# One packed load for seven small inputs, weight splits and a count moved off GpSimd, and the last norms on VectorE

## The chip, the cores and the metric

The kernel runs on 1 core of one Trainium2 chip. A core has five engines that work side by side: PE (TensorE, matrix products), DVE (VectorE), ACT (ScalarE), POOL (GpSimd) and SP (SyncE, which here only starts DMA transfers). Each engine takes its instructions strictly in order; semaphores make one wait for another. Transfers are started from the queues of SP, ACT and POOL. The metric is the device time of the whole program in microseconds; lower is better. The time before is the median of three runs, 4089.68 us, between 4086.54 and 4090.18.

## The reference, cut to what matters

The input is 2048 tokens of 1024 numbers and a condition vector. The program computes one layer of a network. `_layer_norm` is (x − mean)·rsqrt(var + eps).

```python
m = split(silu(c) @ mod_w + mod_b, 6)                       # six rows of 1024
h = _layer_norm(x, 1e-6) * (1 + m[1]) + m[0]
y = _hyena(h, ...)                                          # projection, short and long convolutions, w_out
x = _ln_affine(alpha * x + (1 + m[2]) * y, ln_g[0], ln_b[0])
h = _layer_norm(x, 1e-6) * (1 + m[4]) + m[3]
aff = softmax(h @ w_router)                                 # 2048 x 16
gate, idx = top_k(aff.T, 256)                               # each of 16 experts picks 256 tokens
ye = (silu(xe @ w1) * (xe @ w3)) @ w2 * gate                # xe = h[idx], inner width 2048
x = _ln_affine(alpha * x + (1 + m[5]) * scatter_add(ye), ln_g[1], ln_b[1])
```

The filters of the long convolution come out of a small network with sine activations (`hy_f_w1`, `hy_f_b1`, `hy_f_freq`, ...), and their spectra are needed.

## The kernel before

The program runs through stages on one core. From 0 to some 120 us (the **start**) it forms the first two rows of the modulation (`early_mod`): SP loads 16 tiles `mw` of 128x1024; the products of five of the eight tiles of one half run on PE as columns of `sd` (L462), the rest is accumulated on DVE in `macc` (L467) and summed over partitions by `sd<-ones_f,macc` on PE (L470); L473 adds the bias `mb` and gives `md`, which stands on DVE ahead of the last statistics of the first quarter of the tokens. A tile `mw` has a buffer that PE or DVE must free before SP loads the next into it. Beside it `filter_acts` runs the sine network: products `sp`, `g` (L209), `turn` on ACT (L211), the rounding `kk` on DVE (L213, L214), and the sine `a` or `zt` on ACT (L215). `side_steps` loads the tokens in quarters of 4 tiles, adds the position rows on POOL, takes the statistics on DVE (L376), and `rstd_steps` (L380 to L393) makes 1/sqrt(var + eps): `lva` on DVE, the root on ACT, a Newton step on DVE; `norm` scales the four tiles on ACT (L506). PE then transposes them (L522) and the projection of `_hyena` begins. An order of the instructions at the start is chosen by a scheduler from the code's order and waits.

Then come filters, projection and convolutions up to some 1510 us, and `phase_out` (the product with `w_out`, the norms, the logits of the router) to some 1772, in 20 rounds `n`, written by hand. Beside it `moe_start` is a generator: its first step builds constants and loads the first chunk of the first expert's weights; its second step, run at `n == 16` of `phase_out`, derives `tri` and `blkb`; its third, run in `phase_route` after the exponentials, splits two chunks.

A **split** is how single precision is kept with the faster matmul type: a weight tile (`w1r`, `w3r`, `w2r`, 128x2048 a chunk) is cast to a high half on ACT (`w1h`), and a low half is the difference (`w1l`) from DVE, or at the first two chunks from POOL (L1400, L1401). Each product is then three matmuls.

`phase_route` (L1274) picks the 256 tokens of each expert by a search for the threshold: 15 steps, 7 on the upper and 8 on the lower 16 bits of the weights. A step counts with three DVE instructions (L1320, `junk`, the count in `cnt`) how many of 128x256 values reach three candidates; PE sums the counts over partitions (`cp`, L1322); DVE compares (L1338), and forms the next candidates (`base` L1335, `cand` L1342, `thr` L1324).

`phase_moe` (L1440) then runs the experts. `route(e)` (L1452) finds the indices, gathers 2x128 tokens (`xg`) and transposes them through the PSUM buffer `tp` (one buffer) into `xs` in two halves; `project` makes `ab` (three buffers), `hidden` the product with silu (`u`, `hh`, `hl`), `back` the accumulation `acc`. Experts 0 to 12 are ordered by the scheduler. The **last three experts** (some 3640 to 4065 us) have their order written by hand: each has 16 steps `n` of `project_summed`, `flush` (the `back` of the step before), `hidden`, the splits for the next chunk (two on even steps, one on odd ones), and one turn of each open `settle`. A `settle` takes 256 tokens of the sum of all experts (`accd`), gathered or straight, and does their final norm; the table `plan` says at which step of which expert one opens. Ten are opened. Its steps are: load; nothing; statistics, `va` and the start value of 1/sqrt (L1565 to L1570) on DVE and three Newton rounds on POOL (L1572 to L1577); and the scaling, per 128 tokens one ACT instruction (L1580) and two POOL instructions by `ln_g` and `ln_b` (L1581, L1582). The last expert's own tokens are normed by code at the end that the change leaves alone.

## Time and profile before

| | |
|---|---|
| median of 3 runs | 4089.68 us (4086.54 to 4090.18) |
| profiled execution | 4085.04 us, span 4083.2 us |
| mean granted clock of TensorE | 0.975 |
| busy: PE, DVE, ACT, POOL | 94%, 68%, 48%, 25% |
| chain that ended last: PE, DVE, issue, DMA, POOL, ACT | 75%, 9%, 5%, 4%, 3%, 3% |

The chain is followed back from the last instruction to what released each step. As PE is busy nearly throughout, an instruction of another engine counts only where PE waits for it, and the views by stretch and by wait tell where that is. Times are microseconds from the start of the span unless marked ns.

### The profile page before, as it was taken

To read this page: it belongs to the slowest core of one execution; us is meant where nothing else is said; L and a number is where in the kernel's file an instruction comes from. 1 tells how busy PE (TensorE), PEld (TensorE's weight loads), DVE (VectorE), ACT (ScalarE), POOL (GpSimd) and SP (SyncE) were. 2 spreads that over 40 slices of the span, in tenths; PEclk is the share of its full clock that TensorE was granted. 3 is DMA by queue.
4 is the path that set the end of the run, shared out by engine and by line. 5 is a ranking of instruction groups with operands and counts; after the bars stand their busy time and mean duration, and the time that the engine had idled before them with its cause. 6 is when DMAs were issued, how large, how long until landed. Compare 5 with 4: busy or idle time off the path is not lost.

```text
span 4083.2 us, 52931 instructions
## 1 busy us (share of the span) xinstructions
PE 3833.0 (94%) x19839; PEld 3171.7 (78%) x19839; DVE 2789.9 (68%) x4017; ACT 1940.8 (48%) x2845; POOL 1040.3 (25%) x1092
## 2 busy tenths in 40 slices
PE   4899999999999989939999999999999999999997
PEld 3666766777777877827888888888888888888896
DVE  5777876776877877785666666666666666656766
ACT  3544543333777651114555555555555555544443
POOL 2355552212455442220000000000000000014635
PEclk8999999999999999969999999999999999999999
...
GB/s 201 113 175 173 179 172 210 221 205 227 268 283 278 294 251 203 136 162 167 196 193 209 206 196 188 214 204 195 188 215 203 195 189 213 203 176 221 238 228 159
DMA packets 620796, 831.73 MB, mean 204 GB/s; under 512 B 56627, under 2 KB 506947, under 8 KB 618236
## 3 DMA queue, kind: packets, MB, share of 16 engines
...
q10 hardware_dynamic: 17858, 2.95, 0.5%
...
q14 instruction: 100, 0.82, 0.1%
...
## 4 chain that ended last, share of the span: by engine, by line
PE 75%; DVE 9%; issue 5%; DMA 4%; POOL 3%; ACT 3%; SPq 0%; ACTq 0%; POOLq 0%; DVEq 0%
PE ab L1502 19%; PE ab L1503 10%; PE acc L175 5%; PE acc L176 5%; PE acc L177 5%; PE ip L175 3%; PE ip L177 3%; PE ip L176 3%; PE sp L335 2%; PE xp L854 2%; PE ap L889 2%; PE xp L872 2%; PE op L175 1%; PE op L177 1%; PE op L176 1%
## 5 line engine op out<-in xcount | busy, mean ns | idle before, releaser
L1502 PE MATMUL ab<-xs,w3h 128*128 128x512 f32 x1664 | 600.6, 399 | 0.0
L1502 PE MATMUL ab<-xs,w1h 128*128 128x512 f32 x1664 | 598.2, 399 | 0.0
L1401 DVE TENSOR_TENSOR w2l<-w2r,w2h 128x2048 fp32r<-128x2048 f32 x126 | 297.6, 2362 | 267.0 <-ACT w2h L1400 266.9
L1503 PE MATMUL ab<-xs,w3l 128*128 128x256 f32 x1664 | 468.2, 281 | 0.0
L1503 PE MATMUL ab<-xs,w1l 128*128 128x256 f32 x1664 | 466.6, 280 | 0.0
L175 PE MATMUL acc<-w2h,hh 128*128 128x512 f32 x1024 | 404.1, 395 | 14.3 <-ACT hh L170 13.8
L176 PE MATMUL acc<-w2l,hh 128*128 128x512 f32 x1024 | 402.5, 393 | 0.0
L177 PE MATMUL acc<-w2h,hl 128*128 128x512 f32 x1024 | 399.5, 391 | 0.8 <-DVE hl L171 0.8
L1502 PEld LDWEIGHTS ab<-xs,w3h 128*128 128x128 f32 x1664 | 313.0, 188 | 76.6
L1502 PEld LDWEIGHTS ab<-xs,w1h 128*128 128x128 f32 x1664 | 313.0, 188 | 72.9
...
L1401 DVE TENSOR_TENSOR w1l<-w1r,w1h 128x2048 fp32r<-128x2048 f32 x126 | 301.0, 2389 | 62.7 <-ACT w1h L1400 62.6
L170 ACT CAST hh<-u 128x256 fp32r<-128x256 f32 x256 | 104.1, 407 | 478.6 <-DVE u L1525 478.6
L1503 PEld LDWEIGHTS ab<-xs,w1l 128*128 128x128 f32 x1664 | 314.2, 189 | 7.1
L1506 DVE TENSOR_TENSOR u<-ab,u 128x256 f32<-128x256 f32 x416 | 174.6, 420 | 205.2 <-ACT u L1505 196.8
L1503 PEld LDWEIGHTS ab<-xs,w3l 128*128 128x128 f32 x1664 | 314.8, 189 | 0.0
L1401 DVE TENSOR_TENSOR w3l<-w3r,w3h 128x2048 fp32r<-128x2048 f32 x126 | 292.9, 2324 | 18.7 <-ACT w3h L1400 18.7
L1400 ACT CAST w2h<-w2r 128x2048 fp32r<-128x2048 f32 x128 | 244.1, 1907 | 94.7 <-PE acc L177 86.3
L1400 ACT CAST w1h<-w1r 128x2048 fp32r<-128x2048 f32 x128 | 244.5, 1910 | 80.5 <-PE ab L1502 79.0
L1400 ACT CAST w3h<-w3r 128x2048 fp32r<-128x2048 f32 x128 | 244.5, 1910 | 68.4 <-PE ab L1502 66.3
L1505 ACT COPY u<-ab 128x256 f32<-128x256 f32 x416 | 152.8, 367 | 184.9 <-PE ab L1503 184.8
L175 PE MATMUL ip<-hh,wh 128*128 128x512 f32 x576 | 237.4, 412 | 3.3 <-ACT hh L170 3.3
...
## 6 DMA issues: line engine op xcount, KB each, us to landing
w1r<-in_moe_w_dram SPq DMA_DIRECT2D x128, 1024.0 KB
w3r<-in_moe_w_dram SPq DMA_DIRECT2D x128, 1024.0 KB
w2r<-in_moe_w_dram SPq DMA_DIRECT2D x128, 1024.0 KB
fud<-ev SPq DMA_DIRECT2D x128, 256.0 KB
...
bn<-ao POOLq DMA_DIRECT2D x248, 128.0 KB, 7.2
...
```

What stands on the lines that cost most here:

```text
L170: nc.scalar.copy(hi, raw)
L175: nc.tensor.matmul(out, lhsT=ah, rhs=bh, start=start, stop=False)
L176: nc.tensor.matmul(out, lhsT=ah, rhs=bl, start=False, stop=False)
L177: nc.tensor.matmul(out, lhsT=al, rhs=bh, start=False, stop=stop)
L335: nc.tensor.matmul(p, lhsT=s1[:, th], rhs=hb[th], start=True, stop=(n0 > 0))
L854: nc.tensor.matmul(p[:, i], lhsT=s2[:, 2 * gp + i], rhs=r[:, i], start=True, stop=True)
L1400: nc.scalar.copy(h, raw)
L1401: eng.tensor_tensor(l, raw, f_(h), OP.subtract)
L1502: nc.tensor.matmul(p, lhsT=ws[2 * j][:, k, fs], rhs=xs[:, k], start=(k == 0), stop=False)
L1503: nc.tensor.matmul(p[:, 0], lhsT=ws[2 * j + 1][:, k, fs], rhs=xs[:, k, 0], start=False, stop=(k == 7))
L1505: nc.scalar.copy(u, p[:, 1])
L1506: nc.vector.tensor_tensor(u, p[:, 0], u, OP.add)
```

## The change

It has seven parts.

1. The inputs `c`, the first 2048 of `mod_b`, `hy_conv_w`, `hy_conv_b`, `hy_b_in`, `hy_f_freq`, `hy_f_b1` and `hy_f_b2` are packed by the host into one array of 128x148, loaded by one SP transfer (`small`). The SP loads `cs` and `mb`, six `fb` loads and three `prm` loads on the ACT queue go.
2. `rstd_steps` takes the root on ACT straight from the variance with the eps as a bias, and its Newton step has four instructions with three fused ones, and `nb`; the rounding difference `kk` is now a fused instruction.
3. In `phase_out` the second step of `moe_start` comes at `n == 17`, and with it the load of the table for Exp; that step now casts `w1h`, `w3h` on ACT and subtracts `w1l`, `w3l` on DVE. The split of `w2` and that of the second chunk come when the tokens of expert 0 have been gathered and transposed, on ACT and DVE. POOL splits nothing.
4. In a step of the search the third count is made on ACT as a sum of signs (`cs`), DVE makes two, and the comparison is against a row of limits (`lim`).
5. For expert 0 `route(0, wide=True)` transposes three of its four groups into the `ab` buffers.
6. `settle` does everything but transfers on DVE, in five steps: load; nothing; statistics; Newton and the first 128 tokens' two scalings; the second 128 tokens' two scalings.
7. In `plan`, the third settle of the first of the last experts opens at step 6 instead of 5.

The core of the diff:

```diff
 def rstd_steps(nc, wk, r, nb, stat, eps, n):
 
-    va = wk.tile([128, n], F32, name="lva")
-    nc.vector.tensor_scalar(va, stat[:, :, 1], eps, None, op0=OP.add)
+    nc.scalar.activation(r, stat[:, :, 1], AF.Sqrt, bias=eps)
+    yield 1
     sq = wk.tile([128, n], F32, name="lsq")
-    nc.scalar.activation(sq, va, AF.Sqrt)
-    yield 1
-    nc.vector.reciprocal(r, sq)
-    nc.vector.tensor_tensor(sq, r, r, OP.mult)
-    nc.vector.tensor_tensor(sq, sq, va, OP.mult)
-    nc.vector.tensor_scalar(sq, sq, -0.5, 1.5, op0=OP.mult, op1=OP.add)
-    nc.vector.tensor_tensor(r, r, sq, OP.mult)
+    nc.vector.reciprocal(r, r)
+    nc.vector.scalar_tensor_tensor(sq, stat[:, :, 1], eps, r, op0=OP.add, op1=OP.mult)
+    nc.vector.scalar_tensor_tensor(sq, sq, -0.5, r, op0=OP.mult, op1=OP.mult)
+    nc.vector.scalar_tensor_tensor(r, sq, 1.5, r, op0=OP.add, op1=OP.mult)
     nc.vector.scalar_tensor_tensor(nb, stat[:, :, 0], -1.0, r, op0=OP.mult, op1=OP.mult)
     yield 1
...
-            if n == 16:
+            if n == 17:
+                nc.scalar.activation(wk.tile([128, 1], F32, name="r"), ident[:, 0:1], AF.Exp)
                 next(nxt)
             if n < 16:
...
-                cnt = wk.tile([128, 3], BF16, name="cnt", bufs=2)
-                for k in range(3):
+                cnt = wk.tile([128, 2], BF16, name="cnt", bufs=2)
+                cs = wk.tile([128, 1], BF16, name="cs", bufs=2)
+                sign = wk.tile([128, 256], BF16, name="sign")
+                with nc.allow_low_precision(reason="whole numbers of at most 256"):
+                    nc.scalar.activation(sign, v, AF.Sign, scale=-1.0, bias=cand[:, 2:3], accum_out=cs)
+                for k in range(2):
                     junk = wk.tile([128, 256], U16, name=f"junk{k}")
-                    nc.vector.tensor_scalar(junk, v, cand[:, k:k + 1], 0.0, op0=OP.is_ge, op1=OP.add, accum_out=cnt[:, k:k + 1])
+                    nc.vector.tensor_scalar(junk, v, cand[:, k:k + 1], 0.0, op0=OP.is_lt, op1=OP.add, accum_out=cnt[:, k:k + 1])
                 p = ps.tile([128, 3], F32, name="cp", bufs=2)
-                nc.tensor.matmul(p, lhsT=blkb, rhs=cnt, start=True, stop=True)
+                nc.tensor.matmul(p[:, 2:3], lhsT=blkb, rhs=cs, start=True, stop=True)
+                nc.tensor.matmul(p[:, 0:2], lhsT=blkb, rhs=cnt, start=True, stop=True)
                 if n == steps[0]:
                     nc.vector.memset(t, 0.0)
...
     nc.gpsimd.iota(ii, pattern=[[1, 128]], base=128, channel_multiplier=-1)
     yield
+    hs = [(n, raw, wt.tile(list(raw.shape), F32R, name=n + "h"), wt.tile(list(raw.shape), F32R, name=n + "l")) for n, raw in raws]
+
+    def sub(i):
+        _, raw, h, l = hs[i]
+        nc.vector.scalar_tensor_tensor(l, raw, 1.0, f_(h), op0=OP.mult, op1=OP.subtract)
+
+    for i in range(2):
+        nc.scalar.copy(hs[i][2], hs[i][1])
+    for i in range(2):
+        sub(i)
     nc.vector.tensor_scalar(R.tri, ii, 128.0, None, op0=OP.is_gt)
     nc.vector.tensor_scalar(ii, ii, 15, None, op0=OP.bitwise_and)
     nc.vector.tensor_scalar(R.blkb, ii, 0.0, None, op0=OP.is_equal)
+    R.first = [t for h in hs for t in h[2:]]
     yield
-    R.first = []
-    for n in range(2):
-        R.first.append(split(raws, nc.gpsimd))
-        if n == 0:
-            raws = load(0, 1)
+    nc.scalar.copy(hs[2][2], hs[2][1])
+    yield
+    sub(2)
+    raws = load(0, 1)
+    R.second = split(raws[:2])
+    R.raw = raws[2:]
     yield
 
...
             for q in range(4):
-                p = ps.tile([128, 2, 256], F32, name="tp", bufs=1)
+                p = ps.tile([128, 2, 256], F32, name="ab", bufs=3) if wide and q else ps.tile([128, 2, 256], F32, name="tp", bufs=1)
                 for i in range(2):
                     k = 2 * q + i
...
+            yield
             va = wk.tile([128, 2], F32, name="va2")
             nc.vector.tensor_scalar(va, stat[:, :, 1], LN_EPS, None, op0=OP.add)
             r = wk.tile([128, 2], F32, name="r2")
-            nb = wk.tile([128, 2], F32, name="nb2")
             t = wk.tile([128, 2], F32, name="t2")
             nc.vector.tensor_scalar(t.bitcast(I32), va.bitcast(I32), 1, None, op0=OP.logical_shift_right)
             nc.vector.tensor_scalar(r.bitcast(I32), t.bitcast(I32), -1.0, float(0x5f3759df), op0=OP.mult, op1=OP.add)
             for _ in range(3):
-                nc.gpsimd.tensor_tensor(t, r, r, OP.mult)
-                nc.gpsimd.tensor_tensor(t, t, va, OP.mult)
-                nc.gpsimd.tensor_scalar(t, t, -0.5, 1.5, op0=OP.mult, op1=OP.add)
-                nc.gpsimd.tensor_tensor(r, r, t, OP.mult)
-            nc.gpsimd.tensor_scalar(nb, stat[:, :, 0], -1.0, None, op0=OP.mult)
-            nc.gpsimd.tensor_tensor(nb, nb, r, OP.mult)
-            yield
+                nc.vector.scalar_tensor_tensor(t, r, -0.5, r, op0=OP.mult, op1=OP.mult)
+                nc.vector.tensor_tensor(t, t, va, OP.mult)
+                nc.vector.scalar_tensor_tensor(r, t, 1.5, r, op0=OP.add, op1=OP.mult)
             for j in range(2):
-                nc.scalar.activation(x[:, j], x[:, j], AF.Identity, scale=r[:, j:j + 1], bias=nb[:, j:j + 1])
-                nc.gpsimd.tensor_tensor(x[:, j], x[:, j], gb[:, 0], OP.mult)
-                nc.gpsimd.tensor_tensor(x[:, j], x[:, j], gb[:, 1], OP.add)
+                if j:
+                    yield
+                nc.vector.scalar_tensor_tensor(x[:, j], x[:, j], stat[:, j, 0:1], gb[:, 0], op0=OP.subtract, op1=OP.mult)
+                nc.vector.scalar_tensor_tensor(x[:, j], x[:, j], r[:, j:j + 1], gb[:, 1], op0=OP.mult, op1=OP.add)
                 if idx is not None:
                     nc.gpsimd.indirect_dma_start(out=out[0], out_offset=at(idx, j), in_=x[:, j], in_offset=None)
             if idx is None:
                 nc.gpsimd.dma_start(dst, x)
...
-        plan = {-3: {1: "xh", 3: "xl", 5: "xh"}, -2: {0: "xh", 2: "-xl", 5: "xh"}, -1: {0: "xh", 2: "-xl", 5: "xh", 7: "xl"}}
+        plan = {-3: {1: "xh", 3: "xl", 6: "xh"}, -2: {0: "xh", 2: "-xl", 5: "xh"}, -1: {0: "xh", 2: "-xl", 5: "xh", 7: "xl"}}
```

**ACT at the start.** Before, the three loads of `prm` stand on ACT between the third `turn` and the first sine `a`:

```order
L211 ACTIVATE turn<-g,frq 128x512
L211 ACTIVATE turn<-sp,frq 128x512
L593 DMA prm<-in_hy_conv_w_dram 128x72x1
L594 DMA prm<-in_hy_conv_b_dram 128x24x1
L595 DMA prm<-in_hy_b_in_dram 128x24x1
L215 ACTIVATE a_459<-kk 128x512 x2
```

Now (with buffer numbers, since some rows read alike without them):

```order
L205 DMA fw3_118<-in_hy_f_w2_dram 64x64 x2
L215 ACTIVATE turn_449<-sp_447,frq_133 128x512
L215 ACTIVATE turn_457<-g_455,frq_133 128x512
L215 ACTIVATE turn_465<-sp_463,frq_133 128x512
L219 ACTIVATE a1_446<-kk_451 128x512
L215 ACTIVATE turn_473<-g_471,frq_133 128x512
```

The sine follows `turn` with no load between them.

**PE at the start**, between the modulation's columns and the sums over partitions. Before (`sd<-sg,mw` are columns of the modulation, `fw` the weights of the sine network):

```order
L462 MATMUL sd<-sg,mw 128x1 x8
L209 MATMUL sp<-a_459,fw_119 128x512
L209 MATMUL g<-a_459,fw_119 128x512
L470 MATMUL sd<-ones_f,macc_170 128x1 x8
L470 MATMUL sd<-ones_f,macc_171 128x1 x8
L209 MATMUL sp<-zt,fw_120 128x512
```

Now:

```order
L459 MATMUL sd<-sg,mw 128x1 x8
L213 MATMUL sp<-zt,fw_117 128x512
L213 MATMUL sp<-zt,fw_118 128x512
L213 MATMUL g<-zt,fw_117 128x512
L213 MATMUL g<-zt,fw_118 128x512
L213 MATMUL sp<-zt,fw_117 128x512
L213 MATMUL sp<-zt,fw_118 128x512
L467 MATMUL sd<-ones_f,macc_163 128x1 x8
```

Six products of the third sine layer (`sp`, `g` of `zt`) have moved ahead of the sums of `macc`.

**DVE ahead of the softmax of the router.** Before, after the last scaling `h` of the out stage:

```order
L1191 SCALAR_TENSOR_TENSOR h<-h,r,x 128x1024
L1285 TENSOR_REDUCE mx<-lg 128x16
L1286 TENSOR_TENSOR lg<-lg,mx 128x256
L1289 TENSOR_REDUCE mx<-lg 128x16
L1290 RECIPROCAL mx<-mx 128x16
L1291 TENSOR_TENSOR lg<-lg,mx 128x256
L1297 COPY aff<-lg 128x256
```

Now:

```order
L1187 SCALAR_TENSOR_TENSOR h<-h,r,x 128x1024
L1434 SCALAR_TENSOR_TENSOR w1l<-w1r,w1h 128x2048
L1434 SCALAR_TENSOR_TENSOR w3l<-w3r,w3h 128x2048
L1440 TENSOR_SCALAR tri<-ii 128x128
L1441 TENSOR_SCALAR ii<-ii 128x128
L1442 TENSOR_SCALAR blkb<-ii 128x128
L1283 TENSOR_REDUCE mx<-lg 128x16
L1284 TENSOR_TENSOR lg<-lg,mx 128x256
```

Two splits, and the constants, stand between the last `h` and the softmax; on POOL, where the six subtractions stood behind the constants `kc` and `ii`, two constants `lim` are left, then the gathers `xg` follow.

**DVE in the last three experts.** Before, a settle's step after a step's last split (`w2l`), POOL doing the rounds:

```order
L376 BN_STATS bst<-xs 128x6 x2
L377 BN_AGGR stat_30473<-bst 128x2
L1565 TENSOR_SCALAR va_30482<-stat_30473 128x2
L1569 TENSOR_SCALAR t_30486<-va_30482 128x2
L1570 TENSOR_SCALAR r_30484<-t_30486 128x2
L1525 TENSOR_TENSOR u_30553<-u_30553,ab 128x256
L171 TENSOR_TENSOR hl<-u_30553,hh 128x256
L1401 TENSOR_TENSOR w1l<-w1r,w1h 128x2048
```

Now, a step later than its statistics, the Newton rounds and the scalings:

```order
L1587 SCALAR_TENSOR_TENSOR t_30573<-r_30572 128x2
L1588 TENSOR_TENSOR t_30573<-t_30573,va_30570 128x2
L1589 SCALAR_TENSOR_TENSOR r_30572<-t_30573,r_30572 128x2
L1593 SCALAR_TENSOR_TENSOR xs<-xs,stat_30480,gb 128x1024
L1594 SCALAR_TENSOR_TENSOR xs<-xs,r_30572,gb 128x1024
L1469 TENSOR_SCALAR oh<-slot,lo 128x256
L1470 SCALAR_TENSOR_TENSOR oh<-slot,hi,oh 128x256
L1540 TENSOR_TENSOR u_30639<-u_30639,ab 128x256
L181 TENSOR_TENSOR hl<-u_30639,hh 128x256
L1403 TENSOR_TENSOR w2l<-w2r,w2h 128x2048
```

The first three of these rows stand twice ahead of them as well; nine small instructions and the two scalings of 128x1024 (L1593, L1594) have come from POOL and ACT in between two products `u`.

## Rows read from the trace of the kernel before

**Rows 1.** Page, part 1: busy us (share of the span) xinstructions of each engine.

```profile
PE 3833.0 (94%) x19839; PEld 3171.7 (78%) x19839; DVE 2789.9 (68%) x4017; ACT 1940.8 (48%) x2845; POOL 1040.3 (25%) x1092
```

**Rows 2.** Stretches of the start: us, PE, PEld, DVE, ACT, POOL busy, PEclk, DMA, GB/s.

```profile
10.00:25.00 15.00, 12.59 (x42) 9.48 (x42) 3.10 (x4) 0.72 (x2) 8.20 (x7) 1.00 1.04 361
...
30.00:43.00 13.00, 3.02 (x15) 2.93 (x14) 0.71 (x2) 0.00 (x0) 0.00 (x0) 1.00 0.82 167
...
56.00:80.00 24.00, 9.69 (x35) 8.08 (x36) 19.39 (x30) 5.74 (x7) 10.76 (x9) 0.50 0.58 191
80.00:100.00 20.00, 8.85 (x42) 5.35 (x41) 13.06 (x33) 19.40 (x28) 0.00 (x0) 0.76 0.46 158
```

**Rows 3.** Timeline of the start: start us, us, engine, line, instruction, [idle before].

```profile
25.60 15.20 ACTq L594 DMA_DIRECT2D prm<-in_hy_conv_b_dram  x1
...
43.01 1.15 ACT L215 ACTIVATE a<-kk 128x512 f32<-128x512 f32 x2 [16.61 <-issue]
...
56.78 6.99 PE L470 MATMUL sd<-ones_f,macc 128*128 128x1 f32 x32 [6.04 <-DVE macc L467]
...
67.02 8.04 DVE L383 TENSOR_SCALAR lva<-stat 128x4 f32<-128x4 f32 x1
...
80.55 4.64 ACT L506 ACTIVATE x<-x,nb,r 128x1024 f32<-128x1024 f32 x4 [1.30 <-DVE nb L392]
```

**Rows 4.** Waits of PE, 1740 to 1860 us: total us, times, longest us.

```profile
PE cp L1322 <- DVE junk L1320: 44.4, 13, 13.2
```

**Rows 5.** Timeline of routing and of the first gather, 1763 to 1885 us.

```profile
1772.03 1.28 ACT L1270 ACT_TABLE_LOAD   x1
...
1775.71 4.52 POOL L1401 TENSOR_TENSOR w1l<-w1r,w1h 128x2048 fp32r<-128x2048 f32 x1 [43.18 <-ACT w1h L1400]
...
1776.28 0.48 DVE L1320 TENSOR_SCALAR_CACHE_REDUCE junk<-half,kc 128x256 uint16<-128x256 uint16 x1
...
1780.35 4.35 DVE L1342 SCALAR_TENSOR_TENSOR cand<-num,base 128x3 f32<-128x3 f32 x1
...
1803.39 0.48 DVE L1320 TENSOR_SCALAR_CACHE_REDUCE junk<-half,cand 128x256 uint16<-128x256 uint16 x1
...
1805.34 0.48 DVE L1320 TENSOR_SCALAR_CACHE_REDUCE junk<-half,cand 128x256 uint16<-128x256 uint16 x1
...
1843.66 0.90 PE L1482 MATMUL tp<-ident,xg 128*128 128x128 f32 x3 [1.74 <-DMA xg<-xnd,idx]
```

**Rows 6.** Stretch of the last three experts, columns as in rows 2.

```profile
3640.00:4056.00 416.00, 397.08 (x2761) 369.11 (x2760) 274.96 (x287) 181.27 (x185) 213.00 (x206) 0.99 0.68 227
```

**Rows 7.** Waits of PE, 3640 to 4060 us.

```profile
PE acc L175 <- ACT hh L170: 13.8, 8, 3.3
PE ab L177 <- DVE w1l L1401: 3.6, 4, 1.6
```

**Rows 8.** Lines by form, 3640 to 4056: xcount | busy us, mean ns | idle before.

```profile
L1401 DVE TENSOR_TENSOR w1l<-w1r,w1h 128x2048 fp32r<-128x2048 f32 x22 | 62.8, 2854 | 23.5 <-ACT w1h L1400 23.4
...
L171 DVE TENSOR_TENSOR hl<-u,hh 128x256 fp32r<-128x256 f32 x45 | 29.1, 647 | 21.2 <-ACT hh L170 21.2
...
L1580 ACT ACTIVATE xs<-xs,nb,r 128x1024 f32<-128x1024 f32 x20 | 23.8, 1236 | 38.0 <-POOL nb L1577 38.0
```

**Rows 9.** Timeline: one scaling of the out stage, and a settle, 3790 to 3803 us.

```profile
1748.30 1.28 DVE L1191 SCALAR_TENSOR_TENSOR h<-h,r,x 128x1024 f32<-128x1024 f32 x1
...
3791.88 0.42 DVE L1525 TENSOR_TENSOR u<-u,ab 128x256 f32<-128x256 f32 x1 [1.98 <-ACT u L1520]
...
3794.59 2.29 DVE L1401 TENSOR_TENSOR w1l<-w1r,w1h 128x2048 fp32r<-128x2048 f32 x1 [1.38 <-ACT w1h L1400]
...
3799.00 1.28 DVE L376 BATCH_NORM_STATS2 bst<-xs 128x6 f32<-128x512 f32 x2
...
3801.95 0.17 DVE L1565 TENSOR_SCALAR va<-stat 128x2 f32<-128x2 f32 x1
...
3802.15 0.17 DVE L1569 TENSOR_SCALAR t<-va 128x2 int32<-128x2 int32 x1
```

More of the change, by code (lines that the diff above doesn't have):

```diff
@@ L1588, in phase_moe @@
         nxt, pend = [], []
-        with tc.manual_schedule():
-            for _ in route(0):
-                pass
+        first = route(0, wide=True)
+        next(first)
+        next(R.split_first)
+        next(first)
+        for _ in first:
+            pass
+        next(R.split_first)
+        order.close()
         m5 = cst.tile([128, 1024], F32, name="m5")
@@ L1605, in phase_moe @@
             for fc in range(8):
-                ws = R.first.pop(0) if R.first else R.split(R.load(e, fc))
+                if e == 0 and fc < 2:
+                    ws = (R.second + R.split(R.raw)) if fc else R.first
+                else:
+                    ws = R.split(R.load(e, fc))
                 for i in range(2):
```

57 lines of the change are left out of this document (29 added, 28 removed).

## The prediction

> **What bounds the kernel now.** First the busy shares [rows 1]: PE works 94% of the span, so a change on another engine can only pay where PE stands still. There are 4083.2 − 3833.0 = 250 us of that, and the change touches three places of it. The first is the start: by stretches, DMA moves 361 GB/s from 10 to 25 us but 167 GB/s from 30 to 43, and PE is busy 3.02 of those 13 us [rows 2]. The timeline says why [rows 3]: on the ACT queue the transfer `prm` of line 594, issued at 25.60, holds the queue 15.20 us, and the next ACT instruction, the sine `a` that PE waits for, begins at 43.01 after 16.61 us idle. PE gets to the sums of the modulation (`sd` of line 470) at 56.78 and ends them 6.99 later; on DVE `md` waits for these, with the last statistics of the tokens queued behind it; `lva` runs 67.02 to 75.06, and the first norm `x` stands at 80.55; behind it ACT is busy 19.40 of 20 us [rows 2], so what the norm gains is handed on. The second is routing: the waits of PE from 1740 to 1860 give 44.4 us in 13 waits on the counts on DVE [rows 4]. Of these the timeline puts most into two steps [rows 5]: the first count starts at 1776.28, the count two steps later at 1803.39, though a free step takes 1805.34 − 1803.39 = 1.95. In between POOL subtracts six weight halves of 4.52 us each, and the DVE instruction `cand`, on 3 columns, takes 4.35. The third is the last three experts: 416 us in which PE is busy 397.08, so 18.9 idle; DVE is busy 274.96, POOL 213.00 [rows 6]; 13.8 of PE's waits are on ACT's `hh` and 3.6 on DVE's `w1l` [rows 7].
>
> **Start.** Seven small inputs become one SP transfer, so the nine ACT-queue loads of `fb` and `prm` go. The sine can then begin when its `kk` is there, up to 43.01 − 25.60 = 17.4 us sooner; but the sums at 56.78 also need all of the `mod_w` transfers, and these gain only what the small loads and PE's stop, which frees no buffer, took of the stream: over the 17.4 us a share of (361 − 167)/361 = 0.54, so 9.3 (estimate). [...] Then `lva`, 8.04 us behind POOL's adds, is gone, since the root takes the variance and the eps directly on ACT; and from there to 80.55 stand 5.5 us of six small vector instructions with statistics between them, of which one goes and the root's wait for DVE too: 2.5 (estimate). Sum 9.3 + 8.0 + 2.5 = −20. Bounds: −10 if the next DVE instruction waits for POOL's adds as `lva` did (9.3 and under 1); −29 if the full 17.4 arrives, with 8.0 and 3.5. The packed transfer, 76 KB in rows of 592 bytes on SP ahead of `mod_w`, has no row of its form; a `mod_w` tile of 524 KB takes 1.5 us at 361 GB/s, so 0 to 1.5, against the two small SP loads that it replaces: 0 taken.
>
> **Routing.** (a) POOL's six subtractions are gone. The two disturbed steps took 27.11 us; two free ones take 2 × 1.95 = 3.9, so −23.2. (b) The third count moves to ACT by a sign with a sum: one count of 0.48 leaves DVE in each of 15 steps. The sine takes 0.58 for 512 columns (1.15 for two [rows 3]), so the sign of 256 should end beside the two counts left; then −0.48 × 15 = −7; 0 if ACT's wait for `cand` and its sum come last. I take −3. (c) `w1l` and `w3l` move to DVE ahead of the softmax, 2 × 2.29 [rows 9]; PE and ACT transpose the last tokens and form their logits in those 5 us, until the table load at 1772.03, and need no DVE for it; so 0 of it shows, or +2.5 if the last `h` is late. If that cover is gone it costs the 4.6. (d) The table load, 1.28 us [rows 5], goes from there to before the last turn: −1.3 to 0; I take 0, since the casts queue on ACT too. (e) Sixteen transposes run back to back over four buffers rather than two groups with a wait between; but the gather's arrival (1843.66, 1.74 us behind the DMA [rows 5]) starts both, and the projections that stood between them now come behind: 0, within 1. (f) `w2l`, `w1l`, `w3l` on DVE at the start of expert 0: 3 × 2.29 = 7 us while PE has its first projection to do: +1. Sum −23.2 − 3 + 1 = −25. Bounds −20 (b at 0, c at +2.5) and −29 (b at −7).
>
> **Last three experts.** POOL's 4 instructions of each Newton step, its two scalings per 128 tokens (within the 213 us of [rows 6]) and ACT's 20 × 1236 ns = 24 us [rows 8] go; DVE gets nine small operations and two 1.28 us ones per 128 tokens. The small ones cost their pitch, 3802.15 − 3801.95 = 0.20: the change adds 12 of which 3 were there, 2.4 per settle less 0.6. The large ones have the price of L1191, 1.28 [rows 9], 1.24 pitch, four per settle: 5.0. Added per settle: 6.8, times ten = 68 us. DVE has room: 416 − 275 = 141; and POOL's share that it blocked returns: `w1l` by 22 × (2854 − 2290) = 12.4, `hl` by 45 × (647 − 420) = 10.2 (0.42 is `u`, of one size [rows 9]), and as much again on `w2l`, `w3l` and the small ones: some 40 (estimate). So no bound by sum, but by place. There are 48 steps: 397.08/48 = 8.3 us of PE each, 8.7 with its stalls, 8.5 taken. On an even step DVE is held from 3791.88 (`u`) to 3799.00 (statistics): 7.1, 1.4 free; on an odd step, with one split less (2.3), 5.0, 3.5 free. The settle puts 2.95 (stats, 3799.00 to 3801.95) on its third step, 2.4 + 2.5 on the fourth, 2.5 on the fifth. `hl` of a step is wanted one step later, less silu, product, cast and difference (some 0.42 each, 1.7): a backlog of 6.8 is free, beyond that PE stands. First of the three experts, settles at 1, 3 and 6: step 3 leaves 0, step 4 leaves 3.5, step 5 (2.5 + 2.95 − 3.5) 5.4, step 6 (4.9 − 1.4) 8.9: PE stalls 2.1. Steps 8, 9, 10 add 0.6, 1.4, 1.1, and the routing of the next expert, whose vector work falls in the same steps, I allow 3 more: 8. The same carry gives 9 and 12 for the other two (three and four settles): 29, and 23 to 32 for a Newton step of 1.8 to 2.7. I take 27, since ACT's 24 us gone shorten its part a little: 27 − 18.9 = +8. Bounds: +14 (33 of stalls) and −15 (4 of stalls, as in rival A).
>
> [...]
>
> **Sum.** −20 − 25 + 8 = −37 on the profiled execution of 4085.04 (span 4083.2): 4048. The median of the runs stands 4.64 above it: 4089.68 − 37 = 4052 (rounded).
>
> **The rivals.**
> A. POOL's blocking and ACT's scalings caused the old stalls, and DVE's added work fits into its idle time: of the held 7.1 us 1 or so is a wait for ACT's cast (23.5 us idle before 22 `w1l` [rows 8]); filled, an even step has 2.4 free, the backlog stays near 6.8 and 0 to 4 us of stalls are left, −17. For it: PE's largest wait, `hh`, hangs on ACT [rows 7], which loses 24 us; against: the cast stands behind `hh` on ACT, and so moves with the backlog. 4052 − 8 − 17 = 4027. Chance 0.20.
> B. The change doesn't do at the start what it says: PE's order, half-clocked [rows 2], and POOL's adds hold the norm; −10. For it: the 0.50 stretch; against: the 15.20 us that the queue is held. 4062. Chance 0.15.
> C. [...] Chance 0.04. [...]
> D. Slower. DVE's added work never finds room: every settle's 10.2 us (stats 2.95, Newton 2.4, four 1.24) falls on PE, 102 − 18.9 = +83, the rest −45: 4089.7 + 38 = 4128. It decides once the settles put more on DVE than the free 4.9 per two steps; in an expert's 16 steps that is 39, against 31 to 41 of three or four settles, so only the dependences could do it. Chance 0.04.
> E. B together with half of that, +30 in the last experts: 4089.7 − 10 − 25 + 30 = 4085, not to be told from no change. Chance 0.04.
>
> **How the numbers follow.** Forecast 0.53, A 0.20, B 0.15, C 0.04, D 0.04, E 0.04. A measurement of this kernel can tell about 0.2%, 8 us, from no change. Faster: 0.53 + 0.20 + 0.15 + 0.04 = 0.92, same 0.04, slower 0.04. The range reaches to A's side with the start at −24 (4024), and to B with the stalls at +14 (4070).
>
> **What would show it.** Start: no `prm` on the ACT queue, `a` before 30, `x` of the norm near 60. Routing: no 4 us instruction on 3 columns, 15 steps of 1.6 to 1.95. Last experts: waits of PE on `hh` and `hl` of 27 rather than 18.9, most at the sixth steps. Wrong would be a norm after 70, a step above 2.2, or PE idle above 45 or under 10 in the last 416 us.

## The result: 42 us faster, by other sums than those forecast

The changed kernel took 4048.36 us as the median of 4 runs (4037.83 to 4050.38), the kernel before 4089.93 in the runs beside them (4086.54 to 4093.45). The ratio is 0.9893, with a 95% interval of 0.9874 to 0.9912, or 36 to 52 us. The forecast was 4052, from 4024 to 4070. The profiled execution took 4050.38 us, with a span of 4046.9.

The busy shares of the profile after answer to [rows 1]:

```profile
PE 3844.1 (95%) x19854; PEld 3179.3 (79%) x19854; DVE 2802.0 (69%) x4116; ACT 1927.0 (48%) x2855; POOL 831.1 (21%) x908
```

PE has 3844.1 us of work where it had 3833.0, and POOL 209 us less; the span lost 36.3 us. Where it lost them is read by setting the same instructions of the two traces side by side, and noting how much earlier the one of after starts:

| place | before | after | earlier by |
|---|---|---|---|
| first norm, `x` on ACT | 80.55 | 62.74 | 17.8 |
| median of the instructions from 160 to 200 us | | | 18.9 |
| a scaling `h` near the end of the out stage | 1748.30 | 1739.84 | 8.5 |
| first reduction of the softmax, `mx` | 1772.05 | 1764.75 | 7.3 |
| first count of the search | 1776.28 | 1768.58 | 7.7 |
| second group of gathered tokens on PE, `tp` | 1843.66 | 1809.84 | 33.8 |
| median of the instructions from 1900 to 2000 us | | | 35.3 |
| median of the instructions from 3600 to 3640 us | | | 36.2 |
| end of the span | 4083.2 | 4046.9 | 36.3 |

So in these two traces the start gained 18.9, of which 10.4 were gone by the end of the out stage; the routing gained 25.3 and the first experts 1.5 to 2.4; the last three experts gained nothing.

The stretches of the start, as [rows 2] (us, then PE, PEld, DVE, ACT and POOL busy, granted clock, DMA share and GB/s):

```profile
30.00:43.00 13.00, 13.00 (x33) 8.09 (x33) 10.46 (x15) 5.09 (x8) 0.00 (x0) 1.00 0.56 187
...
43.00:50.00 7.00, 6.38 (x39) 4.68 (x37) 4.74 (x9) 2.33 (x2) 1.79 (x2) 0.99 1.05 379
```

From 30 to 43 us PE is busy 13.00 of 13, where it was 3.02. The timeline after, as [rows 3] (start, duration, engine, line, instruction, idle time before it and its releaser):

```profile
23.64 0.63 ACT L219 ACTIVATE a<-kk 128x512 f32<-128x512 f32 x1 [3.40 <-DVE kk L218]
...
45.75 3.63 PE L467 MATMUL sd<-ones_f,macc 128*128 128x1 f32 x32
...
49.41 0.24 DVE L470 SCALAR_TENSOR_TENSOR md<-sd,small 128x8 f32<-128x8 f32 x2 [2.26 <-PE sd L467]
...
54.88 5.54 DVE L390 SCALAR_TENSOR_TENSOR lsq<-stat,eps,r 128x4 f32<-128x4 f32 x1
...
62.74 3.49 ACT L503 ACTIVATE x<-x,nb,r 128x1024 f32<-128x1024 f32 x3
```

The first sine starts at 23.64, not 43.01; the sums over partitions at 45.75, not 56.78, and they take 3.63 rather than 6.99. The granted clock is 0.99 from 43 to 50 us, after a stretch in which PE never stood. In the kernel before it was 0.50 from 56 to 80 [rows 2], after 6 us in which PE worked for 0.74:

```profile
50.00:56.00 6.00, 0.74 (x2) 0.00 (x0) 6.00 (x9) 0.70 (x1) 0.00 (x0) 0.81 0.93 302
```

The 1.00 of the rows ahead of 43 us must not be read as the fast pace: 16 products of 128x1 take 3.41 us there (at 34.72), 0.21 each, as slow as the 32 at 0.50 (6.99 us, 0.22 each). `lva` is gone, and an instruction behind it, `lsq` on 4 columns, takes 5.54 us.

PE's waits from 1732 to 1825 us, as [rows 4] (total, times, longest), and places of the timeline of routing, as [rows 5]:

```profile
PE cp L1323 <- ACT sign L1318: 19.8, 15, 2.2
```

```profile
1758.65 2.29 DVE L1434 SCALAR_TENSOR_TENSOR w1l<-w1r,w1h 128x2048 fp32r<-128x2048 f32 x1 [1.10 <-ACT w1h L1437]
...
1764.75 0.42 DVE L1283 TENSOR_REDUCE mx<-lg 128x16 f32<-128x256 f32 x1 [0.94 <-ACT lg L1235]
...
1768.58 0.48 DVE L1321 TENSOR_SCALAR_CACHE_REDUCE junk<-half,kc 128x256 uint16<-128x256 uint16 x1
...
1773.69 0.48 DVE L1321 TENSOR_SCALAR_CACHE_REDUCE junk<-half,cand 128x256 uint16<-128x256 uint16 x1
...
1773.77 0.51 ACT L1318 ACTIVATE sign<-half,cand 128x256 bf16<-128x256 uint16 x1 [1.29 <-DVE cand L1344]
...
1775.30 0.48 DVE L1321 TENSOR_SCALAR_CACHE_REDUCE junk<-half,cand 128x256 uint16<-128x256 uint16 x1
...
1809.84 0.90 PE L1497 MATMUL tp<-ident,xg 128*128 128x128 f32 x3 [1.82 <-DMA xg<-xnd,idx]
```

The waits on the counts fell from 44.4 in 13 to 19.8 in 15, none longer than 2.2. A step takes 1775.30 − 1773.69 = 1.61.

The last three experts, as [rows 6], [rows 7] and [rows 8]:

```profile
3604.00:4020.00 416.00, 397.35 (x2763) 369.47 (x2762) 296.28 (x417) 157.70 (x165) 28.86 (x26) 0.99 0.68 227
```

```profile
PE acc L185 <- ACT hh L180: 13.4, 10, 2.8
...
PE ab L187 <- DVE w1l L1403: 3.1, 4, 0.9
...
PE tp L1497 <- DVE xs L1500: 2.1, 1, 2.1
```

```profile
L1403 DVE TENSOR_TENSOR w1l<-w1r,w1h 128x2048 fp32r<-128x2048 f32 x22 | 50.4, 2292 | 30.4 <-ACT w1h L1402 30.4
...
L1594 DVE SCALAR_TENSOR_TENSOR xs<-xs,r,gb 128x1024 f32<-128x1024 f32 x20 | 25.7, 1285 | 0.7
...
L181 DVE TENSOR_TENSOR hl<-u,hh 128x256 fp32r<-128x256 f32 x45 | 19.2, 426 | 21.2 <-ACT hh L180 21.2
...
L1587 DVE SCALAR_TENSOR_TENSOR t<-r 128x2 f32<-128x2 f32 x30 | 4.8, 161 | 1.0
```

PE is idle 18.65 of 416 us, practically the 18.9 before. DVE's splits take 2292 ns rather than 2854 and `hl` 426 rather than 647, as was expected of a POOL that does no arithmetic; DVE's busy time is 296 rather than 275 all the same, with 51 us of scalings in it.

### The profile page after: what moved, and what is told of

The parts are those of the page before. It is cut to its first block, busy times and chain, and to the rows that moved or that the text cites. A ratio compares the mean times of both kernels' runs of the same rounds, so it can differ in the third digit from the quotient of the medians.

```text
span 4046.9 us, 52886 instructions
## 1 busy us (share of the span) xinstructions
PE 3844.1 (95%) x19854; PEld 3179.3 (79%) x19854; DVE 2802.0 (69%) x4116; ACT 1927.0 (48%) x2855; POOL 831.1 (21%) x908
## 4 chain that ended last, share of the span: by engine, by line
PE 75%; DVE 10%; issue 5%; DMA 4%; ACT 3%; POOL 1%; SPq 0%; ACTq 0%; POOLq 0%; DVEq 0%
PE ab L1517 19%; PE ab L1518 10%; PE acc L185 5%; PE acc L186 5%; PE acc L187 5%; PE ip L185 3%; PE ip L187 3%; PE ip L186 3%; PE xp L850 2%; PE xp L868 2%; PE ap L885 2%; PE sp L339 1%; PE op L185 1%; PE op L187 1%; PE op L186 1%
## 5 line engine op out<-in xcount | busy, mean ns | idle before, releaser
L1403 DVE TENSOR_TENSOR w1l<-w1r,w1h 128x2048 fp32r<-128x2048 f32 x127 | 290.9, 2291 | 68.7 <-ACT w1h L1402 68.7
```

The source lines that it names most:

```text
L1403: eng.tensor_tensor(l, raw, f_(h), OP.subtract)
```

## The experiments

Four things had to be told apart: whether the 10 us that the start loses again are the change's own; which of the small loads, or the new root step, brought the first norm forward; what the search gained from which edit; and why the last three experts stand as they stood. The first four runs take the change apart.

### The parts alone

**The start alone**: the packed inputs, the fused rounding and the root step, in the kernel before.

```diff
+            S.small = S.top.tile([128, 148], F32, name="small")
+            nc.sync.dma_start(S.small, A["c_small"])
...
-        nc.scalar.dma_start(prm[:, 0:3], A["hy_conv_w"][0].rearrange("j (k p) -> p j k", p=128))
+        prm = S.small[:, 24:144].rearrange("p (j k) -> p j k", j=5)
...
+    nc.scalar.activation(r, stat[:, :, 1], AF.Sqrt, bias=eps)
```

> The kernel before with the packed small inputs, the fused rounding and the new root step alone; routing, splits and final norms as before. Theory 1 (the norm's 17.8 us at the start are partly given back between 200 and 1560 us, because the work that follows is put in another order and meets new waits, as the shift of -18.9 at 200 and -8.5 at 1600 between the two traces suggests): 8 to 10 us faster, ratio 0.9976 to 0.998, and the wait of g on wh of 3.5 us near 200 us is there again. Theory 2 (what was given back is chance of that one execution): 16 to 19 us faster, ratio 0.9955 to 0.996, and the shift at 1600 is that at 200.

Measured: 4071.18 us against 4089.87, a ratio of 0.9952 (0.9938 to 0.9965), 14 to 25 us. That is theory 2. In its trace the instructions at 160 us are 18.3 earlier, those at 1600 us 12.9. Two facts explain the rest. The profiled execution of before, at 4085.04, is itself 4.9 faster than the median. And the wait of `g` on `wh`, blamed for the loss near 200 us, is absent here, while it stands in a kernel that has the start of before (the one without POOL's arithmetic, below): 3.1 us. So it comes and goes between executions. Over the seven profiled kernels with the new start (but for the root step in one: the changed one, this one, and the ones with the old norms, three counts, the old root, doubled scalings and the rounds on POOL) the shift at 1600 us lies between 8.5 and 14.3, mean 12.0; over three with the start of before, between −2.9 and 0.5, mean −0.9. Some 13 of the 17 to 19 arrive there, in these traces. Whether the last few are given back by the change or by chance, the interval of 14 to 25 leaves open.

**The routing alone**: out stage, splits, search and wide transposes in the kernel before. The plan's 6 for 5 came with it.

```diff
-            if n == 16:
+            if n == 17:
+                nc.scalar.activation(wk.tile([128, 1], F32, name="r"), ident[:, 0:1], AF.Exp)
                 next(nxt)
...
-        R.first.append(split(raws, nc.gpsimd))
...
+        plan = {-3: {1: "xh", 3: "xl", 6: "xh"}, -2: {0: "xh", 2: "-xl", 5: "xh"}, -1: {0: "xh", 2: "-xl", 5: "xh", 7: "xl"}}
```

> The kernel before with the new out stage, routing, splits on ACT and DVE and the wide transposes alone; start and final norms as before. The traces give 25.4 us up to the end of the search and 1.3 behind it: 26 to 27 us faster, ratio 0.9935. Rival (the gain is taken back by the w2 and second chunk's splits on DVE at the start of expert 0): under 20 us, ratio above 0.995.

Measured: 4062.83 us, ratio 0.9931 (0.9918 to 0.9945): 27 us, of 22 to 34. The splits that moved to the start of expert 0 take nothing back: the shift is 22.4 us at the second group of gathered tokens, 23.2 from 1900 to 2000 us and 23.9 from 2500 to 2600.

**The final norms alone**, in the kernel before. What is expected below names the plan's 6 for 5 as well; the kernel that ran kept the 5.

```diff
-                nc.gpsimd.tensor_tensor(t, r, r, OP.mult)
...
+                nc.vector.scalar_tensor_tensor(t, r, -0.5, r, op0=OP.mult, op1=OP.mult)
...
-                nc.scalar.activation(x[:, j], x[:, j], AF.Identity, scale=r[:, j:j + 1], bias=nb[:, j:j + 1])
-                nc.gpsimd.tensor_tensor(x[:, j], x[:, j], gb[:, 0], OP.mult)
-                nc.gpsimd.tensor_tensor(x[:, j], x[:, j], gb[:, 1], OP.add)
+                nc.vector.scalar_tensor_tensor(x[:, j], x[:, j], stat[:, j, 0:1], gb[:, 0], op0=OP.subtract, op1=OP.mult)
+                nc.vector.scalar_tensor_tensor(x[:, j], x[:, j], r[:, j:j + 1], gb[:, 1], op0=OP.mult, op1=OP.add)
```

> The kernel before with the final norms on VectorE and the plan's 6 for 5 alone. The prediction's carry gave +8 us, ratio 1.002. Theory now, from the stalls of 18.7 before and 18.4 after: 0, within 3 us, ratio 0.9993 to 1.0007, with PE's waits in the last three experts spread over ten or so of 0.5 to 3 us.

Measured: 4086.70 us in 11 runs against 4089.87 in 15, ratio 0.9992 (0.9983 to 1.0001): between 7 us faster and none. The carry's +8 is out for these norms with the 5.

**The changed kernel with the final norms of before**: the same diff, the other way. The plan keeps its 6 here, though the expectation says 5.

> The changed kernel with the final norms of before (rounds and scalings on POOL, one scaling on ACT, plan 5). If the norms on VectorE are worth nothing either way: 4048 us, within 4. If the carry were right, which had them cost 8: 4040. If they gain where the rest is changed (rival A): 4064.

Measured: 4046.82 us, ratio 0.9892 to the kernel before (0.9876 to 0.9907), against the 0.9893 of the changed kernel. The two agree: in this kernel the norms' move to DVE is worth nothing that can be measured. The three parts, 18.7 + 27.0 + 3.2 = 49, are more than the 42 of the whole, but lie within its 36 to 52. What the plan's 6 does was not run by itself; in the traces it is small: from the 48th last `hh` to the last one it is 427.9 us with the old norms and the 5, 428.8 with the old norms and the 6, 426.3 with the new norms and the 5, and 427.7 and 426.5 with both new (the changed kernel and the one with the old root).

### The start: which load it was

**prm back**: the three loads of `prm` as before, c, mod_b and fb packed.

```diff
-        prm = S.small[:, 24:144].rearrange("p (j k) -> p j k", j=5)
+        prm = S.top.tile([128, 5, 24], F32, name="prm")
+        nc.scalar.dma_start(prm[:, 0:3], A["hy_conv_w"][0].rearrange("j (k p) -> p j k", p=128))
+        nc.scalar.dma_start(prm[:, 3], A["hy_conv_b"][0].rearrange("(k p) -> p k", p=128))
+        nc.scalar.dma_start(prm[:, 4], A["hy_b_in"][0].rearrange("(k p) -> p k", p=128))
```

> The changed kernel with the three loads of prm (hy_conv_w, hy_conv_b, hy_b_in) as transfers of 4-byte elements on the ACT queue again; the other small inputs stay packed. Theory (these loads hold ACT's queue and crowd the stream of the modulation's weights): a gap of 10 us or more on ACT between two sines, PE waits for it, first norm at 73 to 78 instead of 62.7. Rival (the six fb loads and the two SP loads of 4-byte elements ahead of the weights were the larger part): first norm under 68.

Measured, in its timeline:

```profile
27.18 7.49 ACTq L593 DMA_DIRECT2D prm<-in_hy_conv_b_dram  x1
...
34.72 0.63 ACT L219 ACTIVATE a<-kk 128x512 f32<-128x512 f32 x1 [6.76 <-issue]
...
49.09 6.46 PE L467 MATMUL sd<-ones_f,macc 128*128 128x1 f32 x32 [2.78 <-DVE macc L464]
...
68.58 4.62 ACT L503 ACTIVATE x<-x,nb,r 128x1024 f32<-128x1024 f32 x4
```

The queue is held 7.49 us rather than 15.20, and the norm comes 5.8 later than in the changed kernel. Neither bound of the theory was met; prm alone is a third of the 17.8. Of its delay 3.3 us are a later start of the sums over partitions (49.09 for 45.75), and 2.8 their duration (6.46 for 3.63): here PE had stood 2.78 us ahead of them.

**fb back**: the six loads of the sine network's small inputs as before, the rest packed.

```diff
+    for s in range(2):
+        sl = slice(s * 64, s * 64 + 64)
+        nc.scalar.dma_start(fb[sl, 0:1], A["hy_f_freq"][0].unsqueeze(1))
+        nc.scalar.dma_start(fb[sl, 1:2], A["hy_f_b1"][0].unsqueeze(1))
+        nc.scalar.dma_start(fb[sl, 2:4], A["hy_f_b2"][0].rearrange("i k -> k i"))
```

> The changed kernel with the six fb loads (hy_f_freq, hy_f_b1, hy_f_b2, elements of 4 bytes) on the ACT queue again; prm, c and mod_b stay packed. With prm back alone the first norm came at 68.58 instead of 62.74, 5.8 of the 17.8 us. If the two kinds of load add up, fb makes up most of the rest: first norm at 70 to 75, the first turn on ACT at 20 or later instead of 15.2. If the early transfers hide fb: under 65.

**fb and prm back**: both edits.

> The changed kernel with fb and prm both loaded as before; only c and mod_b stay packed. If fb and prm together are the cause of the late norm: first norm at 78 to 81, and prm holds the queue for 15 us again. If the two loads on SP ahead of the weights (c and mod_b, the weights' first product at 12.41 before and 6.60 after) are worth the rest: 72 to 75.

Measured, in the timelines of the one and the other:

```profile
24.90 0.78 ACT L220 ACTIVATE turn<-sp,frq 128x512 f32<-128x512 f32 x1 [19.08 <-DMA mw<-in_mod_w_dram]
...
44.94 6.98 PE L472 MATMUL sd<-ones_f,macc 128*128 128x1 f32 x32 [3.08 <-DVE macc L469]
...
66.43 4.64 ACT L508 ACTIVATE x<-x,nb,r 128x1024 f32<-128x1024 f32 x4 [1.36 <-issue]
```

```profile
27.26 12.33 ACTq L598 DMA_DIRECT2D prm<-in_hy_conv_b_dram  x1
...
54.16 6.98 PE L472 MATMUL sd<-ones_f,macc 128*128 128x1 f32 x32 [3.23 <-DVE macc L469]
...
75.66 4.64 ACT L508 ACTIVATE x<-x,nb,r 128x1024 f32<-128x1024 f32 x4 [1.36 <-issue]
```

With fb back the first `turn` begins at 24.90 instead of 15.19, but the norm is only 3.7 late. The weights are not later for it: the sums over partitions begin at 44.94, before the 45.75 of the changed kernel. They take 3.4 us longer, after a wait of PE of 3.08, and from `md` to the norm it is 1.1 longer; these make the 3.7. With both it is 12.9 late, more than 5.8 + 3.7; `prm` holds the queue 12.33 us there, and the sums begin at 54.16. The last 80.55 − 75.66 = 4.9 belong to c and mod_b ahead of the weights on SP and to what else the start changes. That is neither of the two numbers expected. No single load was the cause: `prm` costs the norm 5.8 with the rest packed and 9.2 beside fb (75.66 − 66.43).

The norm is not yet the time. These three runs took 4049.66, 4050.38 and 4052.45 us, one execution each, where the four of the changed kernel lie between 4037.83 and 4050.38. At 1600 us they stand 8.2, 6.2 and 4.6 earlier than the kernel before, below the 8.5 to 14.3 of the kernels with all loads packed. So the loads cost something behind the norm too, but how much of the 3.7 to 12.9 arrives at the end is not shown.

**The old root step** in the changed kernel.

```diff
-    nc.scalar.activation(r, stat[:, :, 1], AF.Sqrt, bias=eps)
...
+    va = wk.tile([128, n], F32, name="lva")
+    nc.vector.tensor_scalar(va, stat[:, :, 1], eps, None, op0=OP.add)
```

> The changed kernel with the root step of before (lva on DVE, seven instructions). The prediction had 8.0 + 2.5 us for it: first norm at 73. Theory now (POOL's adds hold one DVE instruction in either form, 8.04 us lva before and 5.54 us lsq after): first norm at 64 to 68, with lva or lsq of 5 to 8 us beside POOL's adds.

Measured:

```profile
52.81 0.33 DVE L387 TENSOR_SCALAR lva<-stat 128x4 f32<-128x4 f32 x1
...
55.52 4.95 DVE L392 TENSOR_TENSOR lsq<-r 128x4 f32<-128x4 f32 x1
...
63.03 4.64 ACT L506 ACTIVATE x<-x,nb,r 128x1024 f32<-128x1024 f32 x4 [0.82 <-DVE nb L396]
```

`lva` itself now takes 0.33: it comes at the end of one of POOL's adds (53.10), and the next four begin at 55.52. `lsq`, two instructions on in the root step, is caught by these instead, for 4.95 us. The norm is 63.03 against 62.74, and the one execution took 4042.01 us, inside the changed kernel's 4037.83 to 4050.38. The root step, for which the prediction had 8.0 + 2.5, is worth 0.3: DVE has one instruction in POOL's way in either form.

### The search: which edit

**Three counts on DVE** in the changed kernel.

```diff
-                    nc.scalar.activation(sign, v, AF.Sign, scale=-1.0, bias=cand[:, 2:3], accum_out=cs)
-                for k in range(2):
+                for k in range(3):
...
-                nc.tensor.matmul(p[:, 2:3], lhsT=blkb, rhs=cs, start=True, stop=True)
-                nc.tensor.matmul(p[:, 0:2], lhsT=blkb, rhs=cnt, start=True, stop=True)
+                nc.tensor.matmul(p, lhsT=blkb, rhs=cnt, start=True, stop=True)
```

> The changed kernel with all three counts of a search step on DVE again and one product, the comparison against limits kept. Theory: a step is 1.945 us as before instead of 1.615, and first count to last comparison takes 25.2 + 13 x 0.33 = 29.5 us. Rival (part of the 0.33 comes from the new comparison, not from the count): a step of 1.75 to 1.85.

Measured, two steps one after the other:

```profile
1784.63 0.48 DVE L1317 TENSOR_SCALAR_CACHE_REDUCE junk<-half,cand 128x256 uint16<-128x256 uint16 x1
...
1786.58 0.48 DVE L1317 TENSOR_SCALAR_CACHE_REDUCE junk<-half,cand 128x256 uint16<-128x256 uint16 x1
```

A step is 1.95, so all of the 0.33 is the count on ACT, none the new comparison. From first count to last comparison it is 30.2 us here, 25.0 in the changed kernel and 51.1 in the kernel before: POOL's splits were worth 20.9, the third count 5.2. In the time of this one execution, 4049.83 us, the 5.2 do not show.

### The last three experts: what makes PE wait

**The kernel before without POOL's arithmetic in the norms** (rounds and both scalings left out, so these tokens aren't normed), ACT's scaling kept (it then waits for no `nb`).

```diff
-                nc.gpsimd.tensor_tensor(x[:, j], x[:, j], gb[:, 0], OP.mult)
-                nc.gpsimd.tensor_tensor(x[:, j], x[:, j], gb[:, 1], OP.add)
```

> The kernel before; the final norms of the last three experts leave out POOL's rounds and its two scalings (the output is not the normed one), ACT's scaling stays. If POOL's blocking of DVE made the 18.7 us of PE's waits there: under 6 us, w1l at 2.29 and hl at 0.43. If ACT's scalings in ahead of hh made them: 12 us or more left.

Measured: no wait of PE is left at all in the 48 steps. The stretch and the lines:

```profile
3640.00:4029.00 389.00, 389.00 (x2761) 366.49 (x2760) 235.65 (x287) 182.94 (x185) 30.14 (x26) 1.00 0.72 242
```

```profile
L1401 DVE TENSOR_TENSOR w1l<-w1r,w1h 128x2048 fp32r<-128x2048 f32 x22 | 50.5, 2294 | 30.4 <-ACT w1h L1400 30.4
...
L1572 ACT ACTIVATE xs<-xs,stat,r 128x1024 f32<-128x1024 f32 x20 | 23.7, 1234 | 0.0
...
L171 DVE TENSOR_TENSOR hl<-u,hh 128x256 fp32r<-128x256 f32 x45 | 19.2, 426 | 21.3 <-ACT hh L170 21.3
```

So POOL's arithmetic made the old stalls, and the 24 us that ACT's scalings take made none of them. The stretch is 389 us long instead of 416: 18.9 us of waits had cost 27. The one execution agrees: 4058.13 us, where the kernel before beside it took 4084.71.

POOL made them in two ways, and this run takes both away together. One is that its large instructions hold DVE: in the trace of before single splits take 4.5 us rather than 2.3. The other is that ACT's scalings wait for POOL's last small one, `nb`: ACT stands for it ten times, 38.0 us in all. `hh` comes behind them on ACT, so PE's longest wait is of this second kind:

```profile
3716.39 2.37 ACT L1580 ACTIVATE xs<-xs,nb,r 128x1024 f32<-128x1024 f32 x2 [6.02 <-POOL nb L1577]
...
3719.06 0.42 DVE L1525 TENSOR_TENSOR u<-u,ab 128x256 f32<-128x256 f32 x1 [5.97 <-ACT u L1520]
...
3719.97 0.80 PE L175 MATMUL acc<-w2h,hh 128*128 128x512 f32 x1 [3.25 <-ACT hh L170]
```

DVE had nothing to do for 5.97 us there. Four of PE's 15 waits, 6.2 us of the 18.7 that these make, follow such a stand of ACT; how the rest divides no run tells.

**The two scalings done twice** in the changed kernel (the tokens come out wrongly scaled): more of DVE's work and nothing else.

```diff
                 nc.vector.scalar_tensor_tensor(x[:, j], x[:, j], stat[:, j, 0:1], gb[:, 0], op0=OP.subtract, op1=OP.mult)
                 nc.vector.scalar_tensor_tensor(x[:, j], x[:, j], r[:, j:j + 1], gb[:, 1], op0=OP.mult, op1=OP.add)
+                nc.vector.scalar_tensor_tensor(x[:, j], x[:, j], stat[:, j, 0:1], gb[:, 0], op0=OP.subtract, op1=OP.mult)
+                nc.vector.scalar_tensor_tensor(x[:, j], x[:, j], r[:, j:j + 1], gb[:, 1], op0=OP.mult, op1=OP.add)
```

> The changed kernel with each of the two scalings done twice (the output is not the normed one): 4 more instructions of 1.23 us per settle on DVE, 49 us in all. Theory (DVE's backlog sets PE's stalls in the last three experts, and these are near full with the settles of the change): the waits rise from 18.4 to some 65 (the carry gives +48), the run is 40 to 50 us longer. Rival (DVE still has room there, and the stalls after hang on ACT's order alone): waits under 30.

Measured:

```profile
3604.00:4069.00 465.00, 413.86 (x2762) 380.93 (x2762) 347.29 (x457) 157.04 (x165) 28.61 (x26) 0.95 0.60 203
```

```profile
PE acc L185 <- ACT hh L180: 45.5, 15, 5.5
```

51 us of waits, and the stretch 49 us longer, 465 for 416: as much as the added work, though DVE is busy 347 of the 465. The one execution took 4098.2 us, some 50 more than the changed kernel. The rival (waits under 30) is out. The expected 65 us of waits were too many; the time came out right by luck, since PE's own busy time rose too, from 397.35 to 413.86 for the same instructions, at a granted clock of 0.95 instead of 0.99.

**The Newton rounds on POOL**, the scalings on DVE: POOL's small instructions come back, its large ones don't. `va` and the start value go back into the step of the statistics.

```diff
-            yield
...
-                nc.vector.scalar_tensor_tensor(t, r, -0.5, r, op0=OP.mult, op1=OP.mult)
-                nc.vector.tensor_tensor(t, t, va, OP.mult)
-                nc.vector.scalar_tensor_tensor(r, t, 1.5, r, op0=OP.add, op1=OP.mult)
+                nc.gpsimd.tensor_tensor(t, r, r, OP.mult)
+                nc.gpsimd.tensor_tensor(t, t, va, OP.mult)
+                nc.gpsimd.tensor_scalar(t, t, -0.5, 1.5, op0=OP.mult, op1=OP.add)
+                nc.gpsimd.tensor_tensor(r, r, t, OP.mult)
+            yield
```

> The changed kernel with the three Newton rounds on POOL as before (12 instructions of 128x2 per settle), in the step of the statistics; the two scalings stay on DVE, a step later. If only POOL's two scalings of 128x1024 blocked DVE before, and DVE's 9 small instructions (1.75 us per settle) are what fills it now: the waits in the last three experts fall from 18.4 to some 7 and the run is 8 to 12 us faster than the changed kernel, ratio to before 0.9865 to 0.987. If POOL's small instructions block DVE too: no gain, 18 us of waits or more, ratio 0.989.

Measured: 4028.02 us, ratio to the kernel before 0.9850 (0.9836 to 0.9863), whose interval lies below that of the changed kernel (0.9874 to 0.9912). It is the fastest of all. The stretch, PE's waits, two lines, and a place of the timeline:

```profile
3598.00:3999.00 401.00, 393.30 (x2760) 367.99 (x2759) 283.41 (x327) 157.88 (x165) 89.49 (x146) 1.00 0.70 235
```

```profile
PE acc L185 <- ACT hh L180: 3.2, 4, 2.1
...
PE ab L187 <- DVE w1l L1403: 2.4, 3, 0.9
...
PE tp L1497 <- DVE xs L1500: 2.1, 1, 2.1
```

```profile
L1403 DVE TENSOR_TENSOR w1l<-w1r,w1h 128x2048 fp32r<-128x2048 f32 x22 | 50.4, 2292 | 30.4 <-ACT w1h L1402 30.4
...
L1587 POOL TENSOR_TENSOR t<-t,va 128x2 f32<-128x2 f32 x30 | 20.5, 684 | 2.4
```

```profile
3644.13 0.19 POOL L1588 TENSOR_SCALAR t<-t 128x2 f32<-128x2 f32 x1
...
3644.26 2.29 DVE L1403 TENSOR_TENSOR w1l<-w1r,w1h 128x2048 fp32r<-128x2048 f32 x1 [1.38 <-ACT w1h L1402]
...
3644.40 2.21 POOL L1589 TENSOR_TENSOR r<-r,t 128x2 f32<-128x2 f32 x1
```

The waits fall to 7.7 us and the stretch to 401, 15 less than in the changed kernel; some 6 of the 20 us between the two medians stand in its trace before that stretch. They differ between executions of the same code: at 3600 us the changed kernel, the ones with the old norms and with doubled scalings, and this one, all alike up to there, stand 36.2, 40.5, 36.3 and 41.9 earlier than the kernel before. POOL does 30 instructions of 684 ns and 90 of 323 to 562 on average beside DVE, and `w1l` still takes 2292. These averages hide two cases: 95 of the 120 take 0.18 to 0.42 us, 84 of them at most 0.21, and the other 25, of 1.1 to 2.2, all end with a split or scaling of DVE that began before them, as `r` at 3644.40 does. So there POOL waits for DVE and not DVE for POOL. Beside POOL's 128x2 operations DVE's `w1l` took its 2292 ns, beside the 128x1024 ones of the kernel before 2854.

## Why the prediction was right, and where it was not

The time was right, within 4 us, and so was the sign. Of its three terms one was right as a sum with two wrong parts, one right by errors that cancel, and one forecast as a loss that did not come. That they add up to the time is luck in part: in the profiled execution only 8.5 of the start's 20 are left at the end of the out stage, and the 8 that the last experts were to lose make up most of that.

**Start: −20 forecast; 17.8 at the norm, 14 to 25 in the time.** The 17.8 have three parts: the sums over partitions begin 11.0 earlier (56.78 to 45.75), they take 3.4 less (6.99 to 3.63), and from `md` to the norm it is 3.4 less (63.80 to 80.55 before, 49.41 to 62.74 after). For the first the step on the transfers' limit had 9.3, near it, but the price came from the 17.4 us of the ACT queue alone, with the two SP loads at nothing; with fb and prm back, c and mod_b still packed, the weights' first product comes 5.5 sooner than before (12.41 to 6.88) and the sums 2.6. The second it had at nothing; in the changed kernel the sums follow six filter products with no idle time and take 0.11 us each, where they took 0.22. For the third, the step on the root, it had 8.0 + 2.5, far too large: the run with the old root gives it 0.3, and the rest comes from a shorter hold, as four of POOL's adds fall on one DVE instruction where six did. The bound that was named, another instruction caught by POOL's adds, is what happened, though the norm did not come out at that bound's 10. Rival B, PE's order half-clocked, came by half: the six filter products that now stand ahead of the sums ran from 37.99 to 45.91, the first four matmuls at 0.94 us each and the last four at 0.47, but the norm was not late for it.

**Routing: −25 forecast, 25.3 in the trace, 27 in the time.** Step (a) miscounted: between the counts at 1776.28 and 1803.39 [rows 5] lie three steps, not two, for there are two more first counts in the trace of before:

```profile
1784.74 0.48 DVE L1320 TENSOR_SCALAR_CACHE_REDUCE junk<-half,cand 128x256 uint16<-128x256 uint16 x1
...
1798.12 0.48 DVE L1320 TENSOR_SCALAR_CACHE_REDUCE junk<-half,cand 128x256 uint16<-128x256 uint16 x1
```

So three free steps, 5.8, were to be taken off 27.1, which gives 21.3, and the run with three counts makes it 20.9 where the prediction had 23.2. Step (b) was −3 and is −5.2, near its bound of −7: the sign takes 0.51, its sum 0.19 more, and both end 0.2 us ahead of the second count, as argued. Step (c) cost 1.2, between its 0 and 2.5: the casts `w1h` and `w3h` stand on ACT ahead of the copies of the last transposes, so the softmax stands only 7.3 earlier where the out stage stood 8.5 earlier. Step (d) gave 0.4, (e) nothing to be seen, and (f), +1, was a gain of 1.5 instead.

**Last three experts: +8 forecast; −0.2 in the trace, −7 to 0 in the time.** The terms were right: a small operation takes 161 ns at a pitch of 0.20, a scaling 1.28, and `w1l` and `hl` return to 2.29 and 0.43. What failed is the carry, which turns DVE's backlog into PE's waits: 27 forecast, 18.4 there. In the run with doubled scalings it added 48 where 33 came, and for the rounds on POOL some 7 were expected and 7.7 came. So it is half too high once the backlog is deep; why, no run tells. The forecast also took the 18.9 us of before as given and left their cause to rival A. They were POOL's, all of them, as the run without its arithmetic shows: partly the blocking that rival A names, partly ACT's stand for `nb`, which no rival has. The added work on DVE put as many back, against rival A's second half. With the two nearly equal the net is nothing. Rival D's 102 us on PE is far off. Nothing that a run shows stands behind rival C's 0.04: the nine small operations keep the pitch of 0.20.

By what POOL's large instructions hold DVE, no run tells; that they do, three places show: the splits `w1l` took 2854 ns on average beside POOL's scalings and 2292 without, `lsq` 5.54 us beside four of POOL's adds, and `cand` of the search 4.35 beside POOL's split of 4.52. POOL's small instructions in the fastest run show the other side: the 25 that fall on a split or scaling of DVE end with it, and the splits stay at 2292.
